# A hybrid decoder layer: buffers, queues and engines of the prompt attention's pair merge

## The chip, the cores and the metric

The kernel runs on one core of a Trainium2 chip. The metric is the device time of one execution in microseconds (us). The core has five engines: PE (TensorE, matrix products), DVE (VectorE), ACT (ScalarE), POOL (GpSimd), and SP (SyncE), which here only issues DMA transfers; POOL and ACT issue some as well. Each engine works through its own list of instructions in order, and waits at an instruction until what it needs is there. Data lies in on-chip SBUF, in PSUM (where PE writes) and in DRAM.

## What is computed

One layer for a prompt of 2048 tokens and for 64 sample tokens, width 1024. A norm and one input projection feed two mixers: dilated window attention (mixer A) and gated linear attention (mixer B). Their concatenated outputs go through the output projection `w_o`, a norm and a residual, and a feed-forward block follows. The change lies in mixer A for the prompt and at the start of `w_o`:

```python
PATTERNS = ((128, 1), (512, 4), (2048, 16))      # (window, dilation)

def combine_patterns(results):
    """Merge pattern outputs with weights proportional to their softmax denominators."""
    outs = jnp.stack([o for o, _ in results], axis=0)
    lses = jnp.stack([l for _, l in results], axis=0)
    w = jax.nn.softmax(lses, axis=0)
    return jnp.sum(w[..., None] * outs, axis=0)

def prompt_attn(q, k, v):
    return combine_patterns([dilated_prompt(q, k, v, w, d) for w, d in PATTERNS])

# in layer():
mixed = jnp.concatenate([o_a.reshape(B, T, -1), o_b.reshape(B, T, -1)], axis=-1) @ w_o
```

Every query reads 128 earlier keys and itself in each of three patterns. Attention has 8 heads of 64.

## The kernel before

The program runs three stages: sweeps over the input projection with mixer B and the sample attention (to about 780 us), prompt attention (to about 1145 us), and the tail with `w_o` and the feed-forward block.

**Precision.** Most products work on numbers split in two: a high part `hi` (a rounded copy, by ACT) and a low part `lo` (what is left, by DVE or POOL). `split` (L65) does both.

**Prompt attention** (`attention`, L983) handles heads in four pairs, `pr` 0 to 3. A pair goes through the three patterns, each in four groups `g`; a group has two units, and one in the third pattern (20 units a pair). A unit (`AtUnit`, L1752) computes scores with PE (`qk_`, L1780), reduces them on DVE (L1781) and exponentiates on ACT (L1786), transposes the probabilities on PE (L1803) and copies them into "apt" buffers in two halves (L1806, through the helper lines L61 and L63), and multiplies with the values (L1820). After the last unit of a group, DVE copies the output to the pattern's accumulator "aop" (L1825 to L1829, shown as L63). There are five accumulators, and a pair needs three. The second and third pattern use queries that POOL has gathered by stride into "aqg" (`at_gather`, L1118).

**Loads.** `at_load` (L1061) brings a pair's queries, keys and their low parts in six steps of two transfers each, on the queues given by `qs`: "a" for ACT, "s" for SP, "p" for POOL. Pair 0's come in pieces: the first from ACT's queue, the others from SP's. The next pair's steps are taken one a group in the first two patterns (L1053). `at_loadv` (L1077) brings values, from SP, two groups ahead.

**The merge** (`at_merge`, L1122) of a pair is a Python generator of which one piece is laid between the groups of the next pair. Its parts:
- softmax statistics of the three patterns are brought into one order by PE (L1127, L1130) and DVE into a temporary "atm" (L1136 to L1145);
- the small steps on 32 columns make the three weights (L1151 to L1166), with one exponential on ACT (L1157) and one reciprocal on DVE (L1164). `em` names the engine of the others: POOL for pairs 0 to 2, DVE for pair 3;
- for pairs 0 to 2 the weights are transposed, copied to "awt", written to DRAM (L1184) and read back spread over partitions as "awb" (L1173), all from POOL's queue. Pair 3 makes them on chip, by POOL and ACT copies (L1206, L1204) and PE transposes (L1208);
- for each of four blocks `cb` of 512 tokens: three products in place (L1209 or L1211), an add (L1215), a sum into the merged block `mo`, called "amo" (L1217), and its store to DRAM (L1219). In pair 3, DVE makes the products, the adds and the last two sums, and POOL the first two sums.

The tag "amo" has one buffer. Temporary, transposed weights and merged blocks share it, except that pair 3's temporary lies in a score buffer ("ass", six of them). The stores of pairs 0 to 2 go out from POOL and those of pair 3 from SP (`ms='ppps'`).

**Output projection, first chunk.** It covers the columns 0 to 527 and reads eight tiles `k` of 128 rows in the order `WORD` = 4, 5, 6, 7 (mixer B), 0, 1, 2, 3 (the pairs of mixer A). `wo_pre` (L1340) loads and splits the first four during pair 3; `wo_x` (L1367) loads the other four from DRAM and splits them. `wo` (L1388) first multiplies the first three weight blocks with all tiles but the last, and then goes on with tile 3.

**Order.** The program is written in one order, but a planner with its own model of durations lays out each engine's list: instructions that its model has ready go ahead of those that wait, and it assigns buffers in the same model. Durations on the chip may differ from the model's, and then an engine waits in an order that was good in the model. `after` adds an order by hand.

Of the kernel before, what the change touches and what calls it, by code (L numbers as in the profile page):

```python
# [10 lines left out]
F32 = mybir.dt.float32  # L11
# [16 lines left out]
H = 264  # L28
# [8 lines left out]
class Layer:  # L37
# [916 lines left out]
        yield  # L954


    AB = dict(mw=1, qg=5, vsb=5, mq='p', klh=1, q=2, v=6, s=6, pt=5, op=5, ps=3, ppt=2, po=2, am=1, skew=(2, 2), man=(), ea=3, ed=5, mp=12, aa=(1, 4, 7, 9, 10), ms='ppps', mv=2, em=1)

    def px(self, name, dt=F32):
        return self.pxpool.tile([128, 2 * H], dt, name=self.n(name), tag="px", bufs=4)  # L960
# [22 lines left out]
    def attention(self):  # L983
        with ExitStack() as ctx:
            self.aq[1] = self.pool(ctx, "at1")
            p = self.ap = self.pool(ctx, "at")
            self.app = self.pool(ctx, "atp", bass.MemoryType.PSUM)
            self.ev = 0
            pend = None
            fifo = []  # L990
            sk = self.AB["skew"]

            def drain(n):
                nonlocal pend
                while len(fifo) > n:
                    if len(fifo) > sk[0]:
                        fifo[-1 - sk[0]].t()
                    un = fifo.pop(0)
                    un.t()
                    un.pv()  # L1000
                    if un.last:
                        for _ in pend or ():
                            pass
                        pend = self.at_merge(un.pr, un.ML, un.OP)

            if self.AB['man']:
                eng = mybir.EngineType
                ctx.enter_context(self.tc.manual_schedule(engines={getattr(eng, e) for e in self.AB['man']}))
            self.vq = []
            self.at_loadv(0)  # L1010
            self.at_loadv(1)
            for _ in self.at_load(0, ((1, 2),), to=self.qk0):
                pass
            rest = self.at_load(0, ((2, 4),), to=self.qk0)
            self.qgn = []
            for _ in range(self.AB["qg"]):
                p.tile([128, 4, 128], F32R, name=self.n("aqg"), tag="aqg", bufs=self.AB["qg"])
            for pat in range(3):
                for _ in range(2):
                    p.tile([128, 16, 4], F32, name=self.n("aml"), tag=f"aml{pat}", bufs=2)  # L1020
            for _ in range(2):
                p.tile([128, 3, 4, 128], F32, name=self.n("awb"), tag="awb", bufs=2)
            p.tile([128, 512], F32, name=self.n("amo"), tag="amo", bufs=1)
            pre = iter(())
            for pr in range(4):
                if pr == 3:
                    self.rctx.close()
                    pre = self.wo_pre()
                qk = self.qk0
                nxt = self.at_load(pr + 1) if pr < 3 else iter(())  # L1030
                ML, OP = [], []
                for pat in range(3):
                    base = 16 * (3 * pr + pat)
                    ml = p.tile([128, 16, 4], F32, name=self.n("aml"), tag=f"aml{pat}", bufs=2)
                    op = p.tile([128, 4, 512], F32, name=self.n("aop"), tag="aop", bufs=self.AB["op"])
                    ML.append(ml)
                    OP.append(op)
                    for g in range(4):
                        if base // 4 + g + 2 < 48:
                            self.at_loadv(base // 4 + g + 2)  # L1040
                        for _ in rest:
                            pass
                        po = [None]
                        nu = 1 if pat == 2 else 2
                        for u in range(nu):
                            fifo.append(AtUnit(self, pr, pat, g, u, nu, qk, base, ML, OP, po))
                            fifo[-1].qk_()
                            drain(sk[1])
                            if pat:
                                next(pre, None)  # L1050
                        if pend is not None and pat < 2:
                            next(pend, None)
                        if pat < 2:  # L1053
                            self.qk0 = next(nxt, self.qk0)
            for _ in pre:
                pass
            drain(0)
            for _ in pend:
                pass
# [62 lines left out]
    def at_merge(self, pr, ML, OP):  # L1122
        nc, p, pp, AB = self.nc, self.ap, self.app, self.AB
# [8 lines left out]
        if pr == 3:  # L1132
            tm = self.aq[1].tile([128, 512], F32, name=self.n("atm"), tag="ass", bufs=AB["s"])
        else:
            tm = p.tile([128, 512], F32, name=self.n("atm"), tag="amo", bufs=1)
        nc.vector.tensor_tensor(tm[:, :256].rearrange("p (o b x) -> p o b x", o=16, b=4),  # L1136
                                pm[:, :256].rearrange("p (o b x) -> p o b x", o=16, b=4),
                                cap(sm, 0, [[0, 16], [1, 4], [0, 4]]), op=ALU.mult)
# [7 lines left out]
                                    tm[:, 256:].rearrange("p (c s r x) -> p r c x s", c=4, s=4, r=4)[:, r],  # L1146
                                    axis=AX.X, op=ALU.add)
        ws = [w[:, 0], ML[1], w[:, 1]]
        em = nc.vector if pr == 3 or not AB["em"] else nc.gpsimd
        mm = p.tile([128, 16, 2], F32, name=self.n("amm"), tag="amm", bufs=1)  # L1150
        nc.vector.tensor_tensor(mm, ws[0][:, :, 0:2], ws[1][:, :, 0:2], op=ALU.min)  # L1151
        nc.vector.tensor_tensor(mm, mm, ws[2][:, :, 0:2], op=ALU.min)
# [14 lines left out]
        last = pr == 3  # L1167
# [10 lines left out]
        if not last:  # L1178
            pt = pp.tile([128, 512], F32, name=self.n("pab"), tag="am", bufs=AB["am"])
            nc.tensor.transpose(pt[:96, :128], awf, self.ident)  # L1180
            wt = p.tile([128, 512], F32, name=self.n("awt"), tag="amo", bufs=1)[:96, :128]
            self.evac(wt, pt[:96, :128], "v")
            wd = self.a["awd"][pr]
            nc.gpsimd.dma_start(wd, wt)  # L1184
            nxt = weights(0)
            for _ in range(AB["mw"]):
                yield
        tags = ("am", "ao", "ao")
        j = 0
        for cb in range(4):  # L1190
# [2 lines left out]
                W = weights(cb)  # L1193
            else:
                W, nxt = nxt, weights(cb + 1) if cb < 3 else None
            mo = p.tile([128, 512], F32, name=self.n("amo"), tag="amo", bufs=1)
            for i in range(3):
                if last:
                    tg = tags[j % 3]
# [10 lines left out]
                else:  # L1210
# [7 lines left out]
                            OP[0][:, :, sl], OP[2][:, :, sl], op=ALU.add)  # L1218
            (dict(p=nc.gpsimd, s=nc.sync, a=nc.scalar)[AB['ms'][pr]]).dma_start(self.a["mixa"][:, pr, 512 * cb:512 * cb + 512],  # L1219
                                                       mo)  # L1220
            if cb < 3:
                yield
        yield
# [116 lines left out]
    def wo_pre(self):  # L1340
        nc, a = self.nc, self.a
# [4 lines left out]
        self.wow, self.xnext = [], [None] * KT  # L1346
        self.wo_w(0)
        yield
        for k in self.WORD[:4]:
            hi, lo = self.hl()  # L1350
            r = self.raw()
            nc.sync.dma_start(r, a["mixb"][:, k - 4, :2 * H])
            for i, e in zip(self.split(hi, lo, r, "v"), self.atl):
                self.after(i, e)
            self.xnext[k] = (hi, lo)
            yield
# [10 lines left out]
    def wo_x(self, c):  # L1367
        nc, a = self.nc, self.a
# [1 line left out]
        w = 2 * H  # L1370
        npr = min(w, S - t0)
        xs = self.xnext = [None] * KT if c else self.xnext
        for k in self.WORD[0 if c else 4:]:
            hi, lo = self.hl()
            r = self.spool.tile([128, w], F32, name=self.n("wx"), tag="wx", bufs=3) if c else self.raw()
            if k < 4:
# [596 lines left out]
```

## Time and profile before

| what | value |
|---|---|
| three runs | 2853.13, 2867.46, 2850.01 us |
| median | 2853.13 us |
| the profiled execution's own time | 2860.6 us |
| its span, first to last instruction | 2858.6 us |
| mean granted TensorE clock | 0.978 |
| HBM read, written | 509.29 MB, 143.94 MB |

A page of the profile gives, for each engine, busy time, share of the span and number of instructions. Rows of waits read: engine and tile that waited, its line, what it waited for, then total us, number of waits and the longest. Rows of the timeline read: start and duration in us, engine, line, operation, output<-inputs, shapes, and in brackets the idle time before it and what ended it. Rows of stretches give from:to, length, then busy us of PE, PEld (weight loads), DVE, ACT and POOL with their instruction counts, the granted TensorE clock, the DMA engines' share and GB/s. Rows of groups give minimum, median and maximum duration in ns. Tile names have their numbers left out; a line can be a helper's, as L63 and L71 (the copies and splits).

### The profile page before, as it was taken

The numbers are of one execution on the slowest core, as the hardware profiler recorded it, in microseconds if no ns is written. First come the engines' busy times: TensorE is split into PE (matmuls) and PEld (weight loads), VectorE is DVE, ScalarE is ACT, GpSimd is POOL, SyncE is SP. The second block draws the span as 40 slices with busy tenths as digits, with TensorE's granted clock in tenths as the row PEclk, the third lists the DMA queues.
The fourth block names the chain that finished last, engine by engine and source line by source line (L and its number), as shares of the span: only waits on it lengthen the run. The fifth ranks groups of instructions, "written<-read, shape, count | busy, mean of one in ns | idle before, by whom it ended". The sixth has DMA issues, their size and how long they took to land. (4 is left out here: it accounts for less than half of the span.)

```text
span 2858.6 us, 58660 instructions
## 1 busy us (share of the span) xinstructions
PE 2726.4 (95%) x22255; PEld 2545.2 (89%) x22255; DVE 1854.4 (65%) x4557; ACT 1279.2 (45%) x2958; POOL 598.6 (21%) x751
## 2 busy tenths in 40 slices
PE   7999999999998988899899999999999999999997
PEld 6788899787877766899799999999999999999997
DVE  7657654443355656456899888776667766666666
ACT  6535433332266765344565544443344433443332
POOL 3424242443324466112210003000020000200001
PEclk9999999999999998999899999999999999999998
DMA  8755445898888655347588758787587875876654
GB/s 296 252 179 188 163 147 168 309 335 321 281 176 177 145 128 111 99 154 268 188 309 300 248 208 308 276 294 266 194 321 282 294 261 192 325 256 218 217 193 146
DMA packets 285657, 657.09 MB, mean 230 GB/s; under 512 B 31856, under 2 KB 82672, under 8 KB 283328
## 3 DMA queue, kind: packets, MB, share of 16 engines
q1 hardware_dynamic: 254880, 576.50, 59.9%
q0 software_dynamic: 13408, 44.99, 5.2%
q10 hardware_dynamic: 17088, 31.86, 3.0%
q8 instruction: 175, 2.87, 0.4%
q14 instruction: 106, 0.87, 0.1%
HBM read 509.29 MB, written 143.94 MB: 229 GB/s over the span
## 5 line engine op out<-in xcount | busy, mean ns | idle before, releaser
L68 ACT ACTIVATE ws<-wr 128x512 fp32r<-128x512 f32 (+1 forms) x482 | 293.4, 616 | 437.0 <-PE pfe L1559 132.5
L90 PE MATMUL pfd<-hh,ws 128*128 128x264 f32 x2816 | 476.2, 285 | 9.2 <-ACT ws L68 5.4
L90 PEld LDWEIGHTS pfd<-hh,ws 128*128 128x128 f32 x2816 | 400.3, 189 | 12.6 <-ACT ws L68 7.0
L71 DVE TENSOR_TENSOR ws<-wr,ws 128x512 fp32r<-128x512 f32 (+1 forms) x482 | 319.7, 669 | 137.4 <-ACT ws L68 134.5
L90 PE MATMUL pfd<-hl,ws 128*128 128x264 f32 x1408 | 303.8, 285 | 0.8 <-DVE hl L71 0.8
L1559 PE MATMUL pfa<-xh,ws 128*128 128x264 f32 x1496 | 292.9, 287 | 6.7 <-ACT ws L68 3.4
L1559 PE MATMUL pfe<-xh,ws 128*128 128x264 f32 x1496 | 289.3, 286 | 0.3 <-DVE u L1546 0.3
L1559 PE MATMUL pfd<-xh,ws 128*128 128x264 f32 x1408 | 288.4, 285 | 0.7 <-DVE up L1546 0.5
L1559 PEld LDWEIGHTS pfa<-xh,ws 128*128 128x128 f32 x1496 | 237.3, 190 | 8.6 <-ACT ws L68 5.1
L1559 PEld LDWEIGHTS pfe<-xh,ws 128*128 128x128 f32 x1496 | 237.1, 190 | 0.6 <-DVE u L1546 0.6
L396 PE MATMUL pv<-wh,xh 128*128 128x256 f32 (+1 forms) x816 | 234.0, 287 | 1.1 <-DVE th L693 1.1
L1559 PEld LDWEIGHTS pfd<-xh,ws 128*128 128x128 f32 x1408 | 231.2, 189 | 1.4 <-DVE up L1546 0.7
L396 PE MATMUL pv<-wl,xh 128*128 128x256 f32 (+1 forms) x816 | 231.5, 284 | 0.0
L396 PE MATMUL pv<-wh,xl 128*128 128x256 f32 (+1 forms) x816 | 230.8, 283 | 0.0
L90 PEld LDWEIGHTS pfd<-hl,ws 128*128 128x128 f32 x1408 | 226.1, 189 | 1.1 <-DVE hl L71 1.0
L1786 ACT ACTIVATE ass<-ass,aml 128x256 f32<-128x256 f32 (+1 forms) x384 | 174.2, 456 | 112.5 <-DVE aml L1781 85.1
L1508 POOL DMA_DIRECT2D xl<-d_xst x52 | 28.6, 551 | 889.1 <-PE pfe L1559 854.9
L1559 PE MATMUL pfd<-xl,ws 128*128 128x264 f32 x704 | 200.6, 285 | 0.0
L1781 DVE CUSTOM_DVE_ANT_0 ass<-pas,atab 128x256 f32<-128x256 f32 (+1 forms) x384 | 128.5, 363 | 90.9 <-PE pas L1780 81.0
L90 PE MATMUL pq<-xh,wh 128*128 128x512 f32 (+2 forms) x480 | 174.4, 370 | 10.1 <-ACT xh L234 7.8
L1559 PE MATMUL pfa<-xl,ws 128*128 128x264 f32 x616 | 176.6, 287 | 0.5 <-DMA xl<-d_xst 0.5
L1559 PE MATMUL pfe<-xl,ws 128*128 128x264 f32 x616 | 175.6, 285 | 0.0
(335 smaller groups left out, 6767.8 us busy)
## 6 DMA issues: line engine op xcount, KB each, us to landing
ws<-d_wst SPq DMA_DIRECT2D x248, 512.0 KB
wr<-in_wu SPq DMA_DIRECT2D x114, 512.0 KB
d_wst<-ws SPq DMA_DIRECT2D x88, 512.0 KB
wr<-in_wd SPq DMA_DIRECT2D x160, 256.0 KB
wr<-in_wt SPq DMA_DIRECT2D x60, 512.0 KB
wh<-d_wbs SPq DMA_DIRECT2D x35, 512.0 KB
wl<-d_wbs SPq DMA_DIRECT2D x35, 512.0 KB
skp<-in_ckt SPq DMA_DIRECT2D x16, 1024.0 KB
```

The source lines that it names most:

```text
L68: h = nc.scalar.activation(hi, src, AF.Copy)
L71: return h, (nc.gpsimd if lo_eng == "p" else nc.vector).tensor_tensor(lo, src, hi.bitcast(F32), op=ALU.subtract)
L90: mm = nc.tensor.matmul(o, ww[:, k, :], xx[:, s0:s0 + n], start=(k == order[0] and i == 0), stop=(k == order[-1] and i == 2))
L396: mm = nc.tensor.matmul(ps[:m, :256], x[:, t0:t0 + m], w[:, k % 4, :], start=(k == 0 and i == 0), stop=(k == KT - 1 and i == 2))
L1508: self.nc.gpsimd.dma_start(t.bitcast(F32), xo[i, z])
L1559: self.lastmm = nc.tensor.matmul(bank[:, :H], w[:, ww, k, :], xx, start=new and k == 0 and j == 0, stop=k == 3 and j == 2, skip_group_chec ...
L1781: red = nc.vector.tensor_tensor_reduce(ssb[:, sc:sc + nk], ps[:, sc:sc + nk], L.amk[self.pat][:, 256 - nk:256], scale=1.0, scalar=3e38, op ...
L1786: ex = nc.scalar.activation(ssb[:, sc:sc + nk], ssb[:, sc:sc + nk], AF.Exp, bias=self.ml[:, idx, h:h + 1], scale=-1.0, accum_out=self.ml[: ...
```

## The change

- "amo" gets two buffers and "apt" four in place of five.
- All merged blocks are stored from POOL's queue (`ms='pppp'`).
- Pair 3's small merge steps (`em`) run on POOL as the others' do.
- Pair 3's merged blocks lie in "ass" buffers. The first, and 16 columns of the second, are split from there into tile 3 of the first projection chunk. `wo_pre` prepares three tiles in place of four, and `wo_x` takes tiles 7, 0, 1 and 2; tile 3 is not loaded again from DRAM.
- The last piece of pair 0's queries and keys is issued from POOL's queue.
- The next pair's load steps are taken in the groups 2 to 7 of the pair in place of 0 to 5.

```diff
-    AB = dict(mw=1, qg=5, vsb=5, mq='p', klh=1, q=2, v=6, s=6, pt=5, op=5, ps=3, ppt=2, po=2, am=1, skew=(2, 2), man=(), ea=3, ed=5, mp=12, aa=(1, 4, 7, 9, 10), ms='ppps', mv=2, em=1)
+    AB = dict(mw=1, qg=5, vsb=5, mq='p', klh=1, q=2, v=6, s=6, pt=4, op=5, ps=3, ppt=2, po=2, am=1, skew=(2, 2), man=(), ea=3, ed=5, mp=12, aa=(1, 4, 7, 9, 10), ms='pppp', mv=2, em=1)
...
-            rest = self.at_load(0, ((2, 4),), to=self.qk0)
+            rest = self.at_load(0, ((2, 4),), "pp", to=self.qk0)
...
-            p.tile([128, 512], F32, name=self.n("amo"), tag="amo", bufs=1)
+            for _ in range(2):
+                p.tile([128, 512], F32, name=self.n("amo"), tag="amo", bufs=2)
...
-                        if pat < 2:
+                        if 2 <= 4 * pat + g < 8:
                             self.qk0 = next(nxt, self.qk0)
...
-            tm = p.tile([128, 512], F32, name=self.n("atm"), tag="amo", bufs=1)
+            tm = p.tile([128, 512], F32, name=self.n("atm"), tag="amo", bufs=2)
...
-        em = nc.vector if pr == 3 or not AB["em"] else nc.gpsimd
+        em = nc.gpsimd
...
-            wt = p.tile([128, 512], F32, name=self.n("awt"), tag="amo", bufs=1)[:96, :128]
+            wt = p.tile([128, 512], F32, name=self.n("awt"), tag="amo", bufs=2)[:96, :128]
...
-            mo = p.tile([128, 512], F32, name=self.n("amo"), tag="amo", bufs=1)
+            if last:
+                mo = self.aq[1].tile([128, 512], F32, name=self.n("amo"), tag="ass", bufs=AB["s"])
+            else:
+                mo = p.tile([128, 512], F32, name=self.n("amo"), tag="amo", bufs=2)
...
+            if last and cb < 2:
+                if cb == 0:
+                    self.xnext[3] = self.hl()
+                o, m = ((0, 512), (512, 2 * H - 512))[cb]
+                self.split(*(t[:, o:o + m] for t in self.xnext[3]), mo[:, :m], "v")
...
-        for k in self.WORD[:4]:
+        for k in self.WORD[:3]:
...
-        for k in self.WORD[0 if c else 4:]:
+        for k in self.WORD if c else self.WORD[3:7]:
```

## The prediction

> **What bounds the kernel now.** I read the page first, then busy time by stretches, then what TensorE waited for between 770 and 1200 us, then the timeline of each engine at the longest waits.
>
> ```profile
> span 2858.6 us, 58660 instructions
> PE 2726.4 (95%) x22255; PEld 2545.2 (89%) x22255; DVE 1854.4 (65%) x4557; ACT 1279.2 (45%) x2958; POOL 598.6 (21%) x751
> ...
> 775.00:1145.00 370.00, 327.04 (x2698) 266.73 (x2696) 222.55 (x946) 238.31 (x876) 179.31 (x203) 0.93 0.66 151
> ```
>
> TensorE is the bound over the whole span, but the change sits in prompt attention (775 to 1145 us) and the start of the output projection. There TensorE is busy 327.0 of 370 us, so 43 us of gaps are the most that attention itself can give. Which gaps they are:
>
> ```profile
> PE pas L1780 <- DVE aml L1781: 11.9, 12, 6.9
> PE pbo L1405 <- DVE xl L71: 9.9, 1, 9.9
> PE pas L1780 <- POOL aqg L1118: 8.6, 1, 8.6
> PE pao L1820 <- DVE aop L63: 6.2, 2, 5.7
> PE pas L1780 <- DMA akl<-d_kl: 4.8, 3, 2.7
> PE pas L1780 <- DMA akh<-d_kh: 3.8, 1, 3.8
> ```
>
> Five places, by the longest single waits: 9.9 us in the projection (tail), 8.6 us for a query gather (gap A), 6.9 us on scores (gap B), 5.7 us for a copy at the end of attention, and 8.6 us for loads at the start. Two of them are seen as stretches with no matmul:
>
> ```profile
> 1055.00:1060.00 5.00, 0.00 (x0) 0.00 (x0) 0.00 (x0) 0.00 (x0) 1.20 (x1) 0.84 0.34 114
> 1060.00:1065.00 5.00, 3.81 (x16) 3.03 (x18) 3.93 (x17) 2.65 (x9) 0.63 (x2) 0.50 0.14 52
> ...
> 1155.00:1160.00 5.00, 0.00 (x0) 0.00 (x0) 0.54 (x1) 0.00 (x0) 1.28 (x1) 0.74 0.14 54
> ```
>
> The granted clock is 0.50 in the 5 us after gap B, so a gap costs some more than its idle time.
>
> **Two merged-block buffers (gap B).** The merge of a pair sums each of four blocks into an "amo" tile on GpSimd and stores it. With one buffer, a sum waits until the store before it has landed:
>
> ```profile
> 1039.25 0.61 POOL L1219 DMA_DIRECT2D d_mixa<-amo  x1
> ...
> 1040.97 2.55 POOL L1215 TENSOR_TENSOR aop<-aop,aop 128x512 f32<-128x512 f32 x2
> 1046.42 1.30 POOL L1217 TENSOR_TENSOR amo<-aop,aop 128x512 f32<-128x512 f32 x1 [2.91 <-DMA d_mixa<-amo]
> ...
> 1052.48 1.28 POOL L1217 TENSOR_TENSOR amo<-aop,aop 128x512 f32<-128x512 f32 x1 [3.90 <-DMA d_mixa<-amo]
> ...
> 1058.80 1.27 POOL L1217 TENSOR_TENSOR amo<-aop,aop 128x512 f32<-128x512 f32 x1 [4.19 <-DMA d_mixa<-amo]
> ...
> 1060.10 0.69 DVE L63 COPY aop<-pao 128x512 f32<-128x512 f32 x1 [8.41 <-POOL amo L1217]
> ```
>
> The last row is the link to TensorE: VectorE reached that copy at 1060.10 - 8.41 = 1051.7 and found its accumulator still held by pair 1's merge, whose last sum ended at 1060.07. VectorE works in order, so the score reductions queued behind the copy, and TensorE waited for them (6.9 us). With two buffers, the second sum can follow the adds (they end at 1043.5): to 1044.8, its store issued by 1045.4. The third needs the first store, landed by 1046.4: to 1047.7. The fourth needs the second store; by the waits of 3.90 and 4.19 us, a store lands 4 us after its issue, 1049.4, so the last sum ends near 1050.7, 1 us before VectorE asks. The 8.4 us go; I take -8.4. What is late next is the merge of pair 2, which moves up with everything else. Bounds: -9.5 (with the slow clock after the gap) and -2, if a store lands late or the planner puts other work between.
>
> **The tail: last block from SBUF, stores on GpSimd.** Pair 3's sums share the one buffer now, two on GpSimd and two on VectorE:
>
> ```profile
> 1136.67 0.40 DVE L1166 TENSOR_TENSOR aaw<-aaw,amm 128x32 f32<-128x32 f32 x3
> 1136.99 2.00 DVE L63 COPY aop<-pao 128x512 f32<-128x512 f32 x2
> ...
> 1152.59 0.68 DVE L1215 TENSOR_TENSOR aop<-aop,aop 128x512 f32<-128x512 f32 x1
> 1159.46 1.07 DVE L1217 TENSOR_TENSOR amo<-aop,aop 128x512 f32<-128x512 f32 x1 [6.20 <-DMA d_mixa<-amo]
> 1163.06 1.10 DVE L1217 TENSOR_TENSOR amo<-aop,aop 128x512 f32<-128x512 f32 x1 [2.53 <-DMA d_mixa<-amo]
> 1163.98 2.56 DVE L71 TENSOR_TENSOR xl<-br,xh 128x528 fp32r<-128x528 f32 x4
> ...
> 1156.05 1.28 POOL L1217 TENSOR_TENSOR amo<-aop,aop 128x512 f32<-128x512 f32 x1 [4.03 <-DMA d_mixa<-amo]
> ```
>
> VectorE is done with products and adds at 1153.3, then idles 6.20 and 2.53 us for stores; the low-half splits that TensorE waits for (9.9 us) stand behind those sums and the first ends at 1163.98 + 2.56/4 = 1164.6. After the change each of the four sums has its own "ass" tile, so no sum waits for a store, and tile 3 of the projection is split from the sums and not from a reload. VectorE after 1153.3: two sums 2.17, the split of 512 columns and of 16 columns 0.64 + 0.2 (an estimate from 2.56/4), the first split from DRAM 0.64: 1156.9. The new order leaves tile 7 to this late group, and TensorE has six 264-column matmuls more to do behind the resume:
>
> ```profile
> L90 PE MATMUL pfd<-hh,ws 128*128 128x264 f32 x2816 | 476.2, 285 | 9.2 <-ACT ws L68 5.4
> ```
>
> At 476.2/2816 = 0.17 us each that is 1.0 us. So the tail gives 1164.6 - 1156.9 - 1.0 = 6.7 us, before the next edit. Tile 3's own split is covered by the products of the first three weight blocks, which need seven other tiles first; if that cover is gone, GpSimd's sum, ScalarE's high half and VectorE's low half, some 2.6 us, stand in VectorE's queue ahead of the splits. The four stores now queue on GpSimd instead of SyncE. What is behind them there: the next sum and the weight copies (L1206) for VectorE's products.
>
> ```profile
> L1219 POOL DMA_DIRECT2D d_mixa<-amo x12: 557/580/613, 930.4 to 1148.2; - x12
> DMA to landing us min/median/max: 2.3/3.4/9.4
> ```
>
> Four issues of 0.58 are 2.3 us of GpSimd time; GpSimd waits 4.03 us here now, which covers them. SyncE loses a wait: the loads behind it go out earlier, and they are not on the path.
>
> **The small merge steps on GpSimd.** Eleven 32-column steps of pair 3 move.
>
> ```profile
> L1155 POOL TENSOR_TENSOR aaw<-aml,amm x3: 242/246/248, 875.7 to 1068.4; 128x32 f32<-128x32 f32 x3
> ...
> L1155 DVE TENSOR_TENSOR aaw<-aml,amm x1: 185/185/185, 1134.9 to 1134.9; 128x32 f32<-128x32 f32 x1
> ...
> 875.46 0.25 POOL L1155 TENSOR_TENSOR aaw<-aw,amm 128x32 f32<-128x32 f32 x1 [9.73 <-DVE amm L1152]
> 879.08 0.67 POOL L1166 TENSOR_TENSOR aaw<-aaw,amm 128x32 f32<-128x32 f32 x3 [1.33 <-DVE amm L1164]
> ```
>
> On GpSimd the chain took 879.75 - 875.46 = 4.3 us for pair 0; on VectorE it took about 2.3 (three steps of 0.185 ahead of an exponential, to 1137.07). The weights come 2.0 us later, but they are used only after TensorE's last value products, which wait for VectorE's copies. VectorE is free of the chain, and those copies, which start at 1136.99 behind it and cost TensorE the 5.7 us, can fill that hole, about 2.0 us earlier. The products start only when these copies are done, so I take -2.0 for the tail, 8.7 together. If the planner leaves the copies behind the chain, the edit costs +2.0. Bounds of the whole tail: -11 (splits put ahead of the sums) and -2.
> [...] The rows here show 246 against 185 ns at 32 columns, 1.3 times. [...]
>
> **Loads from GpSimd and later pair loads (start and gap A).** At the start, the second half of pair 0's queries and keys is issued by SyncE, twelve transfers, behind the value loads:
>
> ```profile
> 789.52 0.61 SPq L1073 DMA_DIRECT2D aqs<-d_qh  x1
> ...
> 796.03 1.37 SPq L1073 DMA_DIRECT2D akl<-d_kl  x2
> ...
> 780.78 0.54 POOL L453 DMA_DIRECT2D out_o_vp<-vs  x1 [2.29 <-DMA akh<-d_kh]
> ```
>
> GpSimd's own stores end at 781.3, so twelve issues of about 0.6 end near 788.5 against 797.4 now, 9 us earlier, and they are queued ahead of the first gathers, which need them anyway. TensorE waits 8.6 us for these loads in all. The transfers themselves must still be moved beside the value loads, so I take -2, with bounds of -6 and +3. The next pair's loads begin two steps later and still end four steps before use, so their own delay is hidden. They move against the merge's weights, which go to DRAM and come back:
>
> ```profile
> 890.97 3.00 POOL L1173 DMA_DIRECT2D awb<-d_awd  x4 [6.96 <-DMA d_awd<-awt]
> 904.59 3.73 POOL L1211 TENSOR_TENSOR aop<-aop,awb 128x512 f32<-128x512 f32 x3 [10.62 <-DMA awb<-d_awd]
> ```
>
> GpSimd waits 6.96 and 10.62 us in order, and the gathers behind the products make gap A. Fewer loads in flight would shorten the first wait to the next quickest landings, about 3 us; the second may stay, for the shifted loads now fall on it. I take -2, bounds -8.6 (A gone) and +8 (A doubled).
>
> **One buffer fewer for transposed probabilities.** A unit fills two; four hold two units.
>
> ```profile
> ACT apt L61: 0.7, 1
> ```
>
> Among those that waited for these TensorE products, a copy into the buffers did so once, for 0.7 us. I take 0, and +3 as the bound.
>
> Sum: -8.4 - 8.7 - 2 - 2 = -21.1 us. The profiled execution took 2860.6, so 2839.5 of its like; the median of the runs is 2853.1, so the forecast is 2832. The stages behind are bound by TensorE, so what the tail gains is kept to the end. A measurement of this kernel can tell about 1%, 28.5 us, from no change; the forecast lies inside that.
>
> **Rivals.**
> *Gap A goes too.* If the weights' round trip is no longer slowed by pair loads, A's 8.6 us go whole and the start gives its full 6: -21.1 - 6.6 - 4 = -31.7, 2821. For it: the 6.96 us wait beside the loads. Against it: the same bytes must move, two steps later, while the second round is under way.
> *Only one of the two large terms comes.* The order on each engine is set by a planner with costs of its own; a sum put behind gathers, or a split of tile 3 put early in VectorE's order, would keep about 8.5 us and the start's 2: -10.5, 2843. Late GpSimd transfers would do the same: at the longest landing, 9.4 against 3.4 us, a start 6 us later eats the start's gain and more.
> [...]
> *Slower.* The shifted pair loads meet the weights' loads in both pair 1 and pair 2: GpSimd, in order, holds the gathers behind products that wait. If the 10.62 us wait doubles in pair 1 and a like one appears in pair 2, TensorE loses 21.2 us, and the start at +3 instead of -2 adds 5: -21.1 + 21.2 + 5 = +5.1, 2858. It decides from 21 us of such waits together. Against it: pair 2's gathers did not hold TensorE at all before.
> *The change does nothing here:* the waits are replaced by the same waits on other engines, 2853.
>
> **Chances.** Forecast 0.50 (own range 2825 to 2839), gap A too 0.20, half 0.20, slower 0.05, nothing 0.05. Faster by over 1% (below 2824.6): the second case and the edge of the first, 0.25. Slower by over 1%: 0.02. Within: 0.73. The range 2816 to 2850 leaves out the last two cases and the low edge of the second, some 0.15.
>
> **What would show it.** Right: the copy at about 1050 no longer waits for a sum; VectorE's two last sums follow its last add without a DMA wait; TensorE's wait in the projection is under 3 us; SyncE issues no mixa store. Wrong: TensorE waiting longer than 9 us for a gather in pair 1 or any in pair 2; the copies of the last accumulators still behind the weight chain; a split of the last block holding VectorE. A gap of 8 us at pair 3's start would refute the buffer argument.

## The result, and the profile after

The changed kernel took 2870.5 us (median of 14 runs, 2862.5 to 2878.4); the kernel before, run beside it, 2862.6 us (14 runs, 2850.0 to 2871.4). The ratio is 1.0034 [1.0021, 1.0048]: 9.7 us slower [6.0, 13.7], where the prediction had 21 us faster. The forecast of 2832 us stood on the median of three runs, 2853.1; the median of fourteen is 2862.6, so 9.5 of the 38 us between forecast and result are the base and not the change. The profiled execution took 2878.4 us, 8 us over its own median; a second profile of the same kernel (label g_after, below) took 2860.4 us. So single differences of a few us between profiles mean little. Before, after and the buffers alone have two profiles each; every other run has one. The profiled execution of u3_both (4375 us at a granted clock of 0.55, where its other eleven took 2849.5 to 2863.2 us) ran in another, slow state and is left out of all times and counts.

What TensorE waited for in attention and at the projection's start, after:

```profile
PE pas L1789 <- POOL aqg L1119: 10.9, 3, 6.5
PE pas L1789 <- DVE aml L1790: 7.6, 11, 4.2
PE pas L1789 <- DMA akh<-d_kh: 7.1, 1, 7.1
PE pas L1789 <- DMA akl<-d_kl: 6.6, 2, 3.6
PE pao L1829 <- DVE aop L63: 3.8, 2, 3.3
...
PE pab L1212 <- ACT awb L1208: 2.5, 1, 2.5
...
PE pbo L1414 <- DVE xl L71: 1.3, 1, 1.3
```

The edits did what they say. The 9.9 us wait in the projection is 1.3 us, and the wait of 6.9 us behind the copy at 1052 us is gone: no sum waits for a store. For pair 1's last sums, after:

```profile
1033.45 1.27 POOL L1221 TENSOR_TENSOR amo<-aop,aop 128x512 f32<-128x512 f32 x1
...
1039.35 0.61 POOL L1223 DMA_DIRECT2D d_mixa<-amo  x1
...
1053.08 2.54 POOL L1221 TENSOR_TENSOR amo<-aop,aop 128x512 f32<-128x512 f32 x2
```

The start got worse: single waits of 7.1 and 3.6 us, in place of 3.8 and 2.7. And the gaps that went were not gained. The busy time by stretches shows why. The stretches run from the first scores to the last merge matmul (here the last matmuls of the merge's statistics, L1130) of pair 0, of pair 1 and of pair 3, and on to the first feed-forward matmul. The columns are length, busy time (and instructions) of TensorE, its weight loads, VectorE, ScalarE and GpSimd, then TensorE's granted clock, DMA share and GB/s. First the profile of before:

```profile
779.86:868.72 88.86, 79.17 (x659) 65.57 (x658) 51.67 (x234) 61.44 (x232) 23.30 (x22) 0.94 0.77 172
868.72:959.74 91.02, 79.00 (x656) 62.61 (x654) 52.51 (x226) 56.32 (x209) 49.72 (x57) 0.94 0.74 162
959.74:1130.56 170.82, 155.30 (x1288) 125.68 (x1288) 107.21 (x456) 118.51 (x433) 99.82 (x114) 0.94 0.58 130
1130.56:1358.09 227.53, 209.88 (x1700) 207.51 (x1700) 132.02 (x227) 89.58 (x181) 35.25 (x90) 0.95 0.50 171
```

and after:

```profile
778.61:870.10 91.49, 77.64 (x652) 65.00 (x651) 50.56 (x229) 59.96 (x226) 27.66 (x30) 0.91 0.79 182
870.10:965.90 95.80, 84.92 (x665) 68.52 (x664) 54.27 (x236) 59.99 (x220) 52.68 (x60) 0.88 0.63 137
965.90:1148.18 182.28, 166.56 (x1285) 134.61 (x1283) 111.60 (x450) 117.93 (x426) 98.90 (x112) 0.88 0.57 125
1148.18:1367.76 219.58, 209.90 (x1700) 208.18 (x1700) 130.66 (x217) 90.44 (x183) 38.15 (x103) 0.96 0.52 175
```

In pairs 2 and 3 TensorE is busy 11.3 us longer for the same matmuls (1288 and 1285 records) at a clock of 0.88 in place of 0.94. So one more quantity is needed beside idle time: **clock loss**, TensorE's busy time times (1 - granted clock), summed over windows of 1.25 us. From first scores to the last merge matmul of pair 3, idle time plus clock loss is 37 + 14 us before and 40 + 35 us after. TensorE ran at half clock for 41 us of this part before, for 85 after. How such a stretch begins and ends, after, pair 1:

```profile
935.00:937.50 2.50, 2.00 (x22) 1.46 (x20) 0.90 (x3) 1.15 (x4) 2.50 (x3) 1.00 0.00 0
937.50:940.00 2.50, 2.06 (x12) 1.31 (x11) 0.85 (x6) 1.27 (x6) 2.04 (x4) 1.00 0.40 120
940.00:942.50 2.50, 2.09 (x13) 1.63 (x14) 1.25 (x7) 1.41 (x6) 2.07 (x2) 0.54 0.24 90
...
950.00:952.50 2.50, 2.50 (x14) 2.48 (x13) 1.34 (x9) 1.60 (x7) 0.11 (x1) 0.50 0.21 41
...
957.50:960.00 2.50, 2.31 (x21) 1.99 (x19) 1.82 (x12) 2.09 (x8) 0.93 (x1) 1.00 0.26 72
```

No wait in the 5 us ahead of the drop is longer than 0.5 us; TensorE is merely busy 80% of the time, waiting for a copy of ScalarE (0.5 us), a reduction of VectorE (0.3 us) and for less. The clock then stays at 0.50 for 17 us, in which four kinds of matmul of 128x128 (two of scores, transposes, value products) take 416 to 457 ns on average, against 275 to 308 in the 20 us before it. In the profiles here these stretches last about 3.4, 6.8, 10.2, 13.7, 17.1 us and so on, multiples of 3.41.

### The profile page after: what moved, and what is told of

Its sections match the earlier page's. It is cut to its first block, busy times and chain, and to the rows that moved or that the text cites. A ratio compares the mean times of both kernels' runs of the same rounds, so it can differ in the third digit from the quotient of the medians.

```text
span 2876.6 us, 58649 instructions
## 1 busy us (share of the span) xinstructions
PE 2743.0 (95%) x22255; PEld 2561.7 (89%) x22255; DVE 1860.1 (65%) x4547; ACT 1281.4 (45%) x2959; POOL 615.9 (21%) x778
## 5 line engine op out<-in xcount | busy, mean ns | idle before, releaser
L90 PE MATMUL pq<-xh,wh 128*128 128x512 f32 (+2 forms) x480 | 173.5, 369 | 10.2 <-ACT xh L234 7.9
```

The source lines that it names most:

```text
L90: mm = nc.tensor.matmul(o, ww[:, k, :], xx[:, s0:s0 + n], start=(k == order[0] and i == 0), stop=(k == order[-1] and i == 2))
```

## The experiments

The first theory (C) is the one above: idle time was removed and clock loss took its place. Its first question is which edit does it: the fewer probability buffers (P), the later pair loads (L), the earlier loads at the start (S), or none, each order of instructions having its own stretches (R). Times are against runs of the kernel before on the same chip; 0.001 of the ratio is 2.86 us.

**The parts alone.** Each takes one edit of the diff into the kernel before.

```diff
- ... v=6, s=6, pt=5, op=5 ...        # a5_pt4: this line alone
+ ... v=6, s=6, pt=4, op=5 ...        # a1_buffers: this line, and "amo" tiles with bufs=2
- if pat < 2:                         # a3_late
+ if 2 <= 4 * pat + g < 8:
```

> The kernel before with one edit: four buffers for transposed probabilities in place of five. In the changed kernel's profile TensorE's idle time in attention is as before (40 against 37 us), but the time at half granted clock grew from 41 to 85 us, some 20 us of loss. Theory P (fewer buffers thin TensorE's supply in the last pattern, and the clock falls there): 8 us or more slower, over 60 us at half clock in attention, small waits of value products for the copies into these buffers. Theory L (the later pair loads do it): within 3 us of before. Theory R (where the clock falls is chance of each order of instructions, no one edit is to blame): anything from -10 to +15, and the profile shows the difference as half-clock time and not as idle time.

1.0004 [0.9994, 1.0014]: +1.1 us, within the interval of nothing. Theory P falls.

> The kernel before with two merged-block buffers and, as memory asks for it, four buffers for transposed probabilities. All theories: the wait of the copy at about 1050 us (8.4 us) is gone. Theory P: what that gives is lost to half clock, 0 to +8 us. Theory L: 6 to 10 us faster. Theory R: no sum can be told ahead, but time differs from before by idle time gone (-8) plus the change in half-clock loss.

0.9995 [0.9983, 1.0007], -1.4 us, though the waits went: 7.5 us of TensorE waiting for reductions, and 12 us from merge to feed-forward part. Of the tail's 9.9 us, which the prediction gave to the tail edits, this is left with the two buffers alone:

```profile
PE pbo L1406 <- DVE xl L71: 1.1, 1, 1.1
```

The lengths of pair 1, pairs 2 and 3, and the stretch up to the feed-forward part, in its two profiles (the second is g_buf):

```profile
867.66:963.01 95.35, 85.64 (x652) 68.22 (x650) 52.81 (x224) 56.58 (x207) 52.41 (x60) 0.86 0.71 149
963.01:1139.70 176.69, 165.62 (x1298) 133.56 (x1298) 108.12 (x459) 121.12 (x433) 100.84 (x116) 0.89 0.58 134
1139.70:1353.59 213.89, 206.32 (x1694) 203.87 (x1695) 130.82 (x226) 89.84 (x181) 30.74 (x85) 0.98 0.53 179
```

```profile
870.49:964.55 94.06, 85.61 (x651) 68.23 (x650) 52.80 (x224) 56.58 (x207) 52.49 (x60) 0.87 0.70 150
964.55:1136.70 172.15, 161.03 (x1292) 129.70 (x1291) 107.47 (x458) 120.93 (x433) 101.05 (x116) 0.92 0.59 135
1136.70:1351.89 215.19, 207.55 (x1701) 205.10 (x1700) 131.12 (x226) 89.53 (x181) 30.74 (x85) 0.98 0.53 179
```

From first scores to the first feed-forward matmul, idle time fell by 17 us (55 and 50 us in the two profiles of before, 38 and 34 here) and clock loss rose by 10 (20 and 26 before, 35 and 31 here). Of the 7 us that are left, 6 are lost in the feed-forward part, 1506.6 and 1506.4 us against 1500.5 and 1500.8, about half of it clock loss again; why there isn't settled.

> The kernel before with one edit: the next pair's loads begin two steps later. Theory L: 8 us or more slower, GpSimd's waits for the merge weights longer in pair 2 (6.3 and 6.1 us in the changed kernel against 2.5 and 4.8 before) and query gathers holding TensorE in pair 2. Theory P: within 3 us of before. Theory R: -10 to +15, told apart as half-clock time.

1.0015 [0.9999, 1.0032], +4.3 us, within the interval of nothing. GpSimd's waits for the merge weights are 31 us in its profile and 34 in that of before, so theory L's mechanism isn't there. That profile is of this kernel's fastest run, 2852.4 us, 14 us under its median, so it doesn't show where the 4.3 us lie.

> The kernel before with the tail edits alone: pair 3's sums in score tiles, the last block split from them, its stores from GpSimd, the last small merge steps on GpSimd. All theories: the 9.9 us wait at the projection's start is gone and the time from the last merge matmul to the projection's end is about 8 us shorter, so 6 to 10 us faster, unless (theory R) another order of instructions moves the half-clock time in attention, by up to 10 us either way.

```diff
+ if last: mo = self.aq[1].tile(..., tag="ass", bufs=AB["s"])   # else one "amo" buffer, as before
+ self.split(..., mo[:, :m], "v")     # blocks 0 and 1 of pair 3
- ms='ppps' ... em = nc.vector if pr == 3 ... ; WORD[:4]
+ ms='pppp' ... em = nc.gpsimd ; WORD[:3]
```

0.9980 [0.9965, 0.9994], -5.7 us. Last merge matmul to first feed-forward matmul: 219.6 us, against 227.5 and 226.1 in the two profiles of before. It has the lowest ratio here; its interval overlaps those of u3_both and i1_behind.

**The loads of pair 0, alone and undone.** u1_late is the changed kernel with the pair loads at their old steps; u2_rest has pair 0's remaining loads on SyncE again; u3_both has both undone.

> The kernel before with one edit: the twelve remaining loads of pair 0 issued by GpSimd. If the edits add up, this one must hold what the others leave of the whole (+9.7 us): the buffers gave -1.4, the later pair loads +4.3, the tail -5.7, so +12. Theory S (only the start is hit, as the changed kernel's trace has it): first scores to the last merge matmul of pair 0 longer by 2 to 4 us, the rest as before, +3. Theory R (half-clock stretches fall by chance of the order of instructions): not to be told, and the difference is half-clock time in pairs 1 to 3.

1.0055 [1.0037, 1.0073]: +15.7 us, one edit, and more than the 12 that the sum left to it. Pair 0 is 3.5 us longer than before, theory S's share.

> The changed kernel with both load edits undone (remaining loads of pair 0 on SyncE again, pair loads at their old steps), so buffers and tail alone. If the edits add up: -1.4 - 5.7 = -7 us against before. Theory R: the sum doesn't hold, because another order has its own half-clock stretches; -12 to +5.

0.9991 [0.9979, 1.0002], -2.6 us [-6.0, +0.6]: the sum of -7 lies just outside. But that sum has an interval of its own, some 5 us either way, so this alone doesn't refute adding up.

> The changed kernel with the pair loads at their old steps. If the edits add up and the later loads cost 4.3 us: +5 us against before. If the loss of the changed kernel comes from the later loads meeting the merge weights: 0 or faster than before, with pair 2's gathers no longer holding TensorE. Theory R: -5 to +12.

1.0035 [1.0021, 1.0049], +10.0 us, the changed kernel's own time: the later pair loads cost nothing there.

> The changed kernel with the remaining loads of pair 0 on SyncE again. Theory S: 3 us less than the changed kernel, +7 us against before. If this edit holds the 12 us that the other edits leave: -3 us against before. In every theory the 8 us gap at the start without scores (783 to 797 us) shrinks to before's.

0.9998 [0.9985, 1.0010], -0.6 us: undoing this one edit gives 10 us back. What it does at the start, after:

```profile
768.51 0.64 POOL L1074 DMA_DIRECT2D aqs<-d_qh  x1
...
776.06 0.59 POOL L1074 DMA_DIRECT2D aqs<-d_qh  x1 [1.16 <-DMA atab<-in_asel]
778.24 0.59 POOL L453 DMA_DIRECT2D out_o_vp<-vs  x1 [1.59 <-DMA aqs<-d_qh]
...
790.12 1.09 POOL L453 DMA_DIRECT2D out_o_vp<-vs  x2 [0.75 <-DMA aqs<-d_qh]
```

```profile
786.08 0.77 PE L1789 MATMUL pas<-akh,aqs 128*128 128x128 f32 x2 [7.13 <-DMA akh<-d_kh]
...
789.96 0.45 PE L1789 MATMUL pas<-akl,aqs 128*128 128x128 f32 x1 [2.90 <-DMA akl<-d_kl]
...
797.63 0.55 PE L1789 MATMUL pas<-akl,aqs 128*128 128x256 f32 x1 [3.65 <-DMA akl<-d_kl]
```

The planner put the loads from 768.5 us on, ahead of and between the value stores, whose last is issued at 790 us and not at 781. GpSimd's issues also wait, up to 1.7 us at a time, for earlier transfers to land. The values' loads and the first keys come late with them: SyncE issues two low parts of keys at 789.4 us and not at 785.6, and the next value loads from 791.5 us and not from 787.0. Before, with the loads on SyncE:

```profile
782.87 0.47 PE L1780 MATMUL pas<-akh,aqs 128*128 128x128 f32 x2 [2.68 <-DMA akl<-d_kl]
799.16 0.38 PE L1780 MATMUL pas<-akl,aqs 128*128 128x256 f32 x1 [0.87 <-DMA akl<-d_kl]
805.10 0.48 PE L1780 MATMUL pas<-akh,aqs 128*128 128x256 f32 x2 [3.85 <-DMA akh<-d_kh]
807.40 0.77 PE L1780 MATMUL pas<-akl,aqs 128*128 128x256 f32 x2 [1.30 <-DMA akl<-d_kl]
```

The last three of these, 6.0 us, are for loads that the edit moves, and they are gone after. All three waits after, 13.7 us, are for earlier pieces, which ScalarE and SyncE issue as before; in the kernel before that is the first row alone, 2.7 us. Pair 0 is 91.5 to 92.8 us in all five profiles with this order and no work added, and 86.8 to 89.0 in the ten that have the loads on SyncE. And the span ends later. The stretch from the end of the last store's issue to the end of the span, before and then after:

```profile
2854.37:2858.60 4.23, 0.00 (x0) 0.00 (x0) 0.00 (x0) 0.00 (x0) 0.00 (x0) 0.50 0.19 64
```

```profile
2869.43:2876.60 7.17, 0.00 (x0) 0.00 (x0) 0.00 (x0) 0.00 (x0) 0.00 (x0) 0.50 0.11 38
```

All eight profiles with these loads on GpSimd have 7.2 to 7.3 us there, all eleven without have 4.2 to 5.1. What is longer is GpSimd's closing DRAIN, the instruction behind its last work (maximum of each row, in ns, before and then after); SyncE's two DRAINs behind the last store start 1.6 to 1.8 us after its issue in both.

```profile
L1954 POOLq DRAIN  x3: 40/93/7417, 2850.4 to 2858.3; - x3
L1963 POOLq DRAIN  x3: 40/102/10437, 2865.4 to 2876.4; - x3
```

In the profiles but h3_end's (below) this DRAIN takes 7.4 us, 0.33 us more with pair 3's four stores on GpSimd, and 2.7 us more with the twelve loads.

**Is it thin supply?** f2_fill adds work and edits nothing else, though the planner lays out the other engines' lists somewhat differently too; f1_chain and f3_tailchain test another term, small GpSimd steps that stretch beside VectorE (0.19 us at their shortest, up to 2.42 beside a busy VectorE in the changed kernel's trace).

```diff
+ for _ in range(2 if self.pat == 2 else 1):                    # f2_fill
      nc.tensor.transpose(ptp[:, len(tl), :], ssb[...], L.ident)
- y = self.rms_cols(..., "p" if pin else "v")                   # f1_chain: changed kernel; f3_tailchain: a4_tail
+ y = self.rms_cols(..., "p" if pin is True else "v")           # and post() passes pin=2
```

> The changed kernel with work added: every transpose of the third pattern is done twice into the same place, 512 more matmuls of some 0.055 to 0.11 us at full clock, 28 to 56 us of records that overlap, about 14 to 28 us of TensorE time if none of it is hidden; the output is unchanged. Theory C (the clock falls to half where TensorE's supply is thin, some 80 to 90% busy over 7 us, and that is where the changed kernel lost 20 us): much of the added work takes the place of short waits and of half-clock time; half-clock time in attention falls from 85 us below 60, and the total is less than 10 us above the changed kernel. If thin supply isn't what lowers the clock: half-clock time stays at 85 us or above and the total is 15 to 30 us above the changed kernel.

1.0041 [1.0026, 1.0056], some 2 us over the changed kernel, for 15 us more of matmul work (busy time at full clock in attention, 311 against 294 and 297 us). Clock loss is 25 us, half-clock time 65; the changed kernel's two profiles have 35 and 25, 85 and 65. Its mean granted clock over all runs is 0.9766, the changed kernel's 0.9714. So by the runs most of the added work took the place of waits and half clock, as theory C has it; the fall below 60 us did not come. The profiles don't show it: attention takes 370.6 us here, and 369.6 and 356.8 us in the changed kernel's two, of which the shorter has the same idle time (36 against 35 us) and clock loss (25).

The traces hold a more direct test. In those of before and after, the granted clock has two values, 0.50 and 1.00, and all its 29 and 37 changes lie on a grid of 3.41 us, to within 0.003 us; so each window of such a grid can be sorted by TensorE's busy share in it. In attention (780 to 1140 us, nineteen profiles), windows at full clock were followed by half clock in 57 of 57 cases where TensorE was busy less than 50%, in 27 of 84 at 50 to 80%, in 27 of 270 at 80 to 95%, and in 6 of 1206 above that. Windows at half clock were followed by full clock in 0 of 101 cases where it was busy less than 75%, in 6 of 96 at 75 to 95%, and in 106 of 189 above that. So thin supply goes with the fall, as theory C has it, and with a clock that stays low once it is low; but half of the 117 falls follow a window in which TensorE was idle for more than half, and at 80 to 95% about one window in ten is followed by a fall.

> The changed kernel with one thing more: the Newton steps of the norm factors in the feed-forward part run on VectorE, not GpSimd. In the changed kernel's trace two of these steps, 128x5 elements, took 2.15 and 2.42 us on GpSimd beside a VectorE without a pause, and TensorE waited 3.95 us for them, where the kernel before waited 0.39; from the first feed-forward matmul to this broadcast it is 4.4 us longer. Theory F (small GpSimd steps held up by VectorE are a term of the loss, and depend only on how the two orders fall beside each other): 4 to 6 us less than the changed kernel, +4 to +6 us against before. If the longer stretch has another cause: within 2 us of the changed kernel (+9.7).

1.0047 [1.0034, 1.0059], no gain. The wait moved from 3.95 to 2.6 us and another of 5.3 us appeared. The rows behind the theory, after:

```profile
1499.23 2.15 POOL L109 TENSOR_SCALAR rcz<-rcz 128x5 f32<-128x5 f32 x1
1501.46 2.42 POOL L110 TENSOR_TENSOR rcy<-rcz,rcy 128x5 f32<-128x5 f32 x1
```

In g_after, the same kernel, TensorE does not wait for them: 131.6 us from the first feed-forward matmul to this broadcast, not 136.2. It is a matter of one execution. Theory F falls.

> The kernel before with the tail edits (pair 3's sums in score tiles, last block split from them, stores and small merge steps on GpSimd) and the norm steps of the feed-forward part on VectorE. The tail alone gave -5.7 us, and its profile still had 4.01 us of TensorE waiting for a small GpSimd step in the feed-forward part. Theory F: -9 to -12 us against before, faster than both kernels. If the two don't add up: -3 to -7.

0.9999 [0.9987, 1.0011], -0.3 us: neither theory F's -9 nor the -3 of the other case came.

**One execution or one order?**

> The changed kernel unaltered, for a second profile: how much of the half-clock time is this kernel's and how much one execution's. Theory R (chance of one execution): the stretches at half clock in pairs 1 to 3 lie elsewhere and their sum differs from 85 us by 15 us or more. If they belong to this order of instructions: the drops at 912, 940, 1032, 1094, 1107 and 1134 us come again within some us, and the sum is within 10 us of 85.

2860.4 us. Drops to half clock came again at 915, 946 and 1038 us (913, 940 and 1032 in the first profile), but pair 3's did not: pairs 2 and 3 took 167.2 us and not 182.3, clock loss 25 and not 35 us. So in these two profiles most of the stretches belong to the order, and some to the execution.

> The kernel before unaltered, for a second profile. Theory R: half-clock time in attention differs from 41 us by 15 us or more, as the same kernel's two profiles differed after the change (85 and 65 us). If the low 41 us belong to this order: within 10 us of 41.

2858.4 us. Half-clock time 53 us in place of 41, between the two answers; none of it in pair 2, as in the first profile. Pair 1 took 95.3 us in place of 91.0.

> The buffers-only kernel unaltered, for a second profile. In the first, the wait for a sum was gone and pair 3 was 7.5 us shorter, but pairs 1 and 2 were 4.4 and 13.4 us longer, nearly all of it half-clock time, and the median was only 1.4 us under before. If pair 2's length belongs to this order of instructions: 90 us or more again. If it is one execution's: 78 to 86 us.

2860.1 us. Pair 2's merge again came 91 us behind pair 1's, with 20 us at half clock: it belongs to the order. Its rows stand above.

**Whose queue, and which place?** h1_act puts the twelve loads on ScalarE; i1_behind and i2_tailbehind hold them on GpSimd behind the value stores, as the prediction had them; h3_end has sixteen other GpSimd loads.

```diff
- rest = self.at_load(0, ((2, 4),), "pp", to=self.qk0)
+ rest = self.at_load(0, ((2, 4),), "aa", to=self.qk0)          # h1_act
+ if qs == "pp": self.after(ld, self.lastvp)                    # i1_behind; i2_tailbehind: on a4_tail
+ (nc.gpsimd if c < 2 else nc.sync).dma_start(r, a["xn"][...])  # h3_end, on the kernel before
```

> The changed kernel with the twelve remaining loads of pair 0 issued by ScalarE, right behind the first pieces that it issues there already, and ahead of its first exponentials. Theory E (early transfers crowd out the first pieces, whoever issues them): pair 0 stays at 91 to 93 us from first scores to last merge matmul, +4 to +10 us against before. Theory G (it is GpSimd's queue, where the loads stand among stores): pair 0 back at 87 to 89 us, the end after the last store's issue back from 7.2 to under 5 us, and -3 to +2 us against before.

1.0025 [1.0011, 1.0039], +7.2 us; pair 0 95.1 us; the end 4.5 us. Early transfers cost at the start from ScalarE too, where they also hold its first exponential from 782 to 798 us, so it isn't theory E alone. The start's loss doesn't need GpSimd's queue; the end's does.

> The kernel before with sixteen loads of the feed-forward part issued by GpSimd in place of SyncE, far from attention. In all profiles with twelve more GpSimd loads at the start, the span ends 7.2 to 7.4 us after the last store's issue; in those without, 4.2 to 5.0. Theory N (the number of GpSimd transfers of the whole program sets it): 7 us or more here. If it belongs to the place or the pattern of those twelve: 4.2 us.

The end took 5.1 us, and GpSimd's closing DRAIN 8.3 us, 0.9 more than before: sixteen transfers here cost a third of what those twelve do, so the number alone doesn't make it. (2873.3 us, a single run.)

> The changed kernel with the twelve loads of pair 0 still on GpSimd, but held behind its five stores of values, the place that the prediction gave them. Theory Q (the place in the queue cost the start): the waits of 7.1, 2.9 and 3.7 us for first keys at 783 to 798 us are gone, pair 0 takes 85 to 88 us from first scores to last merge matmul (the prediction's -2 against 88.9), and the time is 5 to 10 us under the changed kernel, 0 to +4 against before. Theory E (more transfers in flight early cost whatever their place): pair 0 at 90 us or more, +6 to +10 against before. The end after the last store's issue: 7.2 us if loads on GpSimd at this stage make it, under 5 if their early place does.

0.9988 [0.9966, 1.0009], -3.4 us, some 13 us under the changed kernel. But the start did not do what theory Q says: pair 0 took 89.9 us, and one wait of 8.55 us for keys came in place of three. (The profile is of a run of 2873.2 us, 13 us over this kernel's median.)

```profile
781.57 0.77 PE L1791 MATMUL pas<-akh,aqs 128*128 128x128 f32 x2 [2.67 <-DMA akl<-d_kl]
...
799.12 0.55 PE L1791 MATMUL pas<-akl,aqs 128*128 128x256 f32 x1 [8.55 <-DMA akl<-d_kl]
```

The end stayed at 7.2 us, so the early place doesn't make it.

> The kernel before with the tail edits and the twelve loads on GpSimd behind the stores. The tail alone gave -5.7 us. Theory Q: a further -1 to -3 from the start, -6 to -9 against before, the fastest here, unless the longer end takes 3 us back. Theory E: the start costs 3 us, -3 to 0 against before.

1.0042 [1.0023, 1.0060], +12.0 us: the same edit, 17.7 us over the tail alone. Here pair 0 is as short as the prediction had it, and the loss is behind it:

```profile
779.39:866.52 87.13, 79.47 (x652) 65.63 (x651) 50.13 (x229) 59.75 (x226) 30.30 (x34) 0.92 0.83 184
866.52:967.08 100.56, 88.00 (x657) 71.19 (x656) 53.13 (x229) 58.40 (x213) 48.90 (x56) 0.81 0.66 144
967.08:1142.72 175.64, 162.54 (x1292) 131.16 (x1291) 107.07 (x457) 120.54 (x432) 99.83 (x114) 0.91 0.55 123
```

Pair 1 at a clock of 0.81. Both theories about the place fall as the cause of the whole.

## Why the prediction was wrong, point by point

- **Two buffers, -8.4: missed by 7 us.** The wait went, as worked out. But the sum took a wait removed as time gained, with the clock as a small bonus ("a gap costs some more than its idle time"). The buffers alone measured -1.4 [-4.9, +2.0]: idle time fell by 17 us, even the tail's wait with it, and 10 us of it went to clock loss, 6 to the feed-forward part. So the sum also added two terms that overlap: 8.4 and 8.7 make 17.1, and the buffers alone take away that much idle time, because pair 3's sums, too, waited for stores with one buffer. The tail edits on top remove no more of it (35 us up to the feed-forward part in u2_rest, 38 and 34 with the buffers alone). The planner's order changes with every edit, in attention a quarter of the windows at full clock have TensorE busy less than 95%, and whether one of them falls to half clock decides over 2 to 12 us at a time (half of a stretch of 3.4 to 24 us at half clock). Over 15 kernels (all but f2_fill) the median time follows the mean granted clock: 0.971 to 0.973 for the six slowest, 0.974 to 0.977 for the others, 3.3 us for 0.001, correlation -0.93. It is no proof by itself: idle stretches lower this mean too (the clock is 0.50 in the 4.2 and 7.2 us behind the last store's issue, in which no engine is busy), and 0.001 of the clock can be worth at most 2.9 us of a span of 2860. The single dips cannot be read off the profile of before.
- **Loads of pair 0 from GpSimd, -2 with bounds -6 and +3: the step that failed most.** Wrong in sign and place. The step had the issues behind the stores that end at 781.3; the planner put them ahead. It took 8.6 us of waits as waits for these loads, but 2.7 of them, at 782.9 us, are for an earlier piece; and it priced an issue at 0.6 us with no wait (where the stores do go first, in i1_behind, the twelve take 10.3 us and not 7.2). Measured +15.7 alone, and 10.3 back when undone. Of this the traces show 3 us in pair 0, where waits for earlier pieces grew from 2.7 to 13.7 us against the 6.0 that went, and 3 us behind the last store, where the prediction priced nothing. The rest is spread: in a2_rest clock loss up to the feed-forward part is 30 us against 20 and 26 before, and the feed-forward part is 7 us longer without the end, a length on which two profiles of the changed kernel differ as much (1501.7 and 1494.4 us up to the last store's issue). The place that the step assumed was then tried: it gives -3.4 us in one surrounding and +12.0 in the other. So the place alone isn't the cause. Why one order has more half clock than another stays open; so does why these twelve loads lengthen GpSimd's last DRAIN.
- **The tail, -8.7: right alone, but not on top of the buffers.** 7.2 us from the last merge matmul to the feed-forward part, by the mean of two profiles each; -5.7 [-10, -1.7] alone. The 6.7 us for sums and splits came (7.2); the 2.0 for the small steps did not. The copies moved up into the hole, as worked out, but the eleven steps took 6.7 us and not 4.3: pair 2's last sum and two stores stand between them. The products begin 12.5 us after the last merge matmul, 12.3 before.

```profile
1152.35 0.25 POOL L1156 TENSOR_TENSOR aaw<-aw,amm 128x32 f32<-128x32 f32 x1 [14.30 <-DVE amm L1153]
...
1152.99 1.29 POOL L1221 TENSOR_TENSOR amo<-aop,aop 128x512 f32<-128x512 f32 x1
1154.21 0.56 POOL L1223 DMA_DIRECT2D d_mixa<-amo  x1
...
1158.33 0.67 POOL L1167 TENSOR_TENSOR aaw<-aaw,amm 128x32 f32<-128x32 f32 x3 [1.73 <-DVE amm L1165]
```

- **Later pair loads, -2 (-8.6 to +8), and one buffer fewer, 0 (+3): within their bounds.** +4.3 alone but nothing when undone; +1.1 [-1.7, +4.0].
- **The rival that was slower** named the pair loads meeting the merge weights. GpSimd's waits for those weights are 25.5 + 14.1 us in attention after and 24.9 + 14.0 with the loads at their old steps: it was not that. TensorE did wait for a gather in pair 2, which the prediction names as a mark of being wrong, but for 1.2 us, and in pair 3 for 3.2; with the old steps it is 0.4 and 3.5.

The parts as measured alone add up to -1.4 + 4.3 - 5.7 + 15.7 = +12.9 us against +9.7, inside their intervals. That is partly luck: the buffers and the tail remove the same idle time, and i2_tailbehind against i1_behind shows that such sums need not hold.

## What to carry to other kernels

Where TensorE has short waits for other engines all along, price a removed wait by what the granted clock does as well: compare idle time and clock loss apart, and take at least two profiles of each kernel, since one execution moves by 15 us. Before adding up two edits, ask whether they remove the same wait. Loads issued earlier are only earlier if nothing needed first stands behind them; where a planner orders the queues, read its order before counting on a place. Time each edit alone: here a tail edit worth 5.7 us was buried under a load edit that cost twice that.

## What the runs showed of the hardware

- TensorE's clock fell to 0.50 with no wait over 0.5 us (80% busy over 5 us) and stayed for multiples of 3.41 us, 17 us in the stretch shown. In attention, over nineteen profiles, 3.41 us at full clock with TensorE busy less than 50% were always followed by half clock (57 of 57), and 3.41 us at half clock with it busy less than 75% never by full clock (0 of 101).
- GpSimd steps of 128x5 elements, 0.19 us at their shortest, took up to 2.42 us beside a VectorE without a pause.
- Twelve loads issued by GpSimd at 768 to 790 us lengthened its closing DRAIN, 2080 us later, by 2.7 us (7.4 to 10.1 in a2_rest, where they are the only edit), wherever in its queue they stood (the end took 7.2 us in i1_behind too); from ScalarE they didn't (4.5 us in h1_act). Four stores added 0.33 us, sixteen other loads 0.9. SyncE's DRAINs behind the last store start as soon after its issue as before (1.6 to 1.8 us). Not explained.
